# Low halves of streamed weights: a VectorE subtraction against a ScalarE negative with a DMA that adds

## The chip, the core and the metric

The kernel runs on one core of a Trainium2 chip. The metric is the device time of one execution in microseconds (us). The engines are named as the profile names them: PE is TensorE (PEld its weight loads), DVE is VectorE, ACT is ScalarE, POOL is GpSimd, SP is SyncE, which issues nearly all DMAs.

## What is computed

One layer of a decoder trunk with 1024 tokens and a model width of 1024, all in float32. A normed input is projected to six streams; an S5 branch (a complex diagonal state space model) and an RG-LRU branch (a causal convolution, two gates per head, a linear recurrence) run side by side; their outputs are merged by sigmoid gates, projected by `w_out`, normed, added to the input, and a gated projection of a second input `p` is added. Cut to what matters here, which are the products with weights:

```python
h = rms_norm(x, g_pre)
s5_x, s5_g, lru_x, lru_g, gate_s, gate_l = jnp.split(h @ w_in, IN_SPLITS, axis=-1)
y_s = s5_ssm(s5_x, ...)
glu_a, glu_b = jnp.split(jax.nn.gelu(y_s) @ w_glu, 2, axis=-1)
z_s = (glu_a * jax.nn.sigmoid(glu_b) * jax.nn.silu(s5_g)) @ w_bs
y_l = rg_lru(causal_depthwise_conv(lru_x, conv_w, conv_b), w_a, b_a, w_x, b_x, lam)
z_l = (y_l * jax.nn.silu(lru_g)) @ w_bl
merged = jax.nn.sigmoid(gate_s) * z_s + jax.nn.sigmoid(gate_l) * z_l
x = x + rms_norm(merged @ w_out, g_post)
x = x + (p @ w_ple) * jax.nn.sigmoid(x @ w_ple_gate)
```

## The kernel before

**Products in halves.** A float32 product is made of three fast ones. Each operand is split into a high half, which is the value rounded to the format of TensorE's fast mode (float32r), and a low half, which is the rest. `three` (L307) issues high x high (L309), high x low (L310) and low x high (L311) into one PSUM bank, each a matmul of 128x128 weights with 512 columns.

**The weight stream.** All weights lie in DRAM as 128x128 blocks in the order of use. `weight_plan` makes 207 quads of them, up to four blocks each (16 quads have two). SP loads them in chunks of up to eight blocks into four raw buffers (`wraw`, and one small buffer for chunks of two blocks). `make` (L212) gives each quad a slot of a ring of six (`wq`): ScalarE copies the raw quad into the high half (L221), rounding it. The low half is owed: `lows` (L225) lets VectorE subtract the high half from the raw quad (L228). `ahead`, called before each quad is used, converts up to four quads ahead, then lets the low halves follow up to one quad behind that, then fetches chunks up to eight quads further, then forms sums two quads further. `fetch` (L165) issues a chunk's load in the program only when a raw buffer's last quad has been converted and is no longer owed.

**Sums of quads.** The products with `w_bs` and `w_out` use Strassen's scheme, in which some weights are sums of blocks: S1, S2, S3, S4. GpSimd forms them (`sum`, L178 to L210; the add at L193). S1 and S2 have one tile each, S4 is written over S2, and S3 over a raw buffer. For `w_out` four quads form a group, S2, S3, S1 and S4, and a group's S1 and S2 are formed only once the group before has been converted (L185).

**The stages**, by their time in the profile: start, `p @ w_ple`, the first norm, and the S5 inputs (0 to 100 us); 18 output rows of `w_in` with the S5 scan as background work (100 to 290); ten heads of the RG-LRU (290 to 575); the S5 gates, `w_glu` and `w_bl` (575 to 750); `w_bs` by Strassen (750 to 793); `w_out` by Strassen (793 to 871), where each of four groups has the products oY, oZ, oW and oV; the norm and `w_ple_gate`, first for one half of the tokens, then for the other (871 to 993). Background work is written as generators, and `tick` takes one step of each after a quad's matmuls.

**Order.** The order of the instructions on PE, DVE, ACT and POOL is that of the code, and each engine takes its own in that order; SP's DMAs are ordered as they are issued in the program. An instruction that waits holds up all behind it on its engine. Waits are set by the framework from what each instruction reads and overwrites: a ring slot may be rewritten when TensorE has used it, a raw buffer or a sum's tile when its readers are done.

Of the kernel before, what the change touches and what calls it, by code (L numbers as in the profile page):

```python
# [9 lines left out]
F32 = mybir.dt.float32  # L10
F32R = mybir.dt.float32r
I32 = mybir.dt.int32
AF = mybir.ActivationFunctionType
ALU = mybir.AluOpType
# [121 lines left out]
class Weights:  # L136
    RING = 6
    RAW = 4

    def __init__(self, ctx, tc, src):  # L140
        self.nc = tc.nc
        self.src = src
        self.rawp = ctx.enter_context(tc.tile_pool(name="wraw", bufs=self.RAW))
        self.tmp = ctx.enter_context(tc.tile_pool(name="wtmp", bufs=1))
        self.ring = ctx.enter_context(tc.tile_pool(name="wring", bufs=self.RING))
        self.raws = {}
        self.live = [[], []]
        self.loads = 0
        self.fetched = 0
        self.ready = []  # L150
        self.done = []
        self.owed = []
        self.sums = {}
        self.pos = 0
# [10 lines left out]
    def fetch(self, upto):  # L165
        while self.fetched <= min(upto, len(QUADS) - 1):
# [3 lines left out]
            live = self.live[small] = [i for i in self.live[small] if i >= len(self.done) - len(self.owed)]  # L170
            if need + len(live) > (1 if small else self.RAW):
                return
# [39 lines left out]
    def make(self, upto):  # L212
        nc = self.nc
        while len(self.done) <= min(upto, len(QUADS) - 1):
            i = len(self.done)
            self.sum(i)
            src, n = self.ready[i]
            t = self.ring.tile([P, 2, 4, P], F32R, tag="q", name=f"wq{i}")
            hi = t[:, 0].rearrange("p b m -> p (b m)")[:, :n * P]
            lo = t[:, 1].rearrange("p b m -> p (b m)")[:, :n * P]  # L220
            nc.scalar.activation(hi, src, AF.Copy)  # L221
            self.owed.append((i, lo, src, hi))
            self.done.append(t)

    def lows(self, upto):  # L225
# [1301 lines left out]
```

## Time and profile before

| what | value |
|---|---|
| time, median of 3 runs | 996.49 us (992.3 to 997.97) |
| the profiled execution, its own time | 995.16 us |
| its span, first to last instruction | 993.4 us |
| granted TensorE clock, mean | 0.988 |
| L228, the subtractions, of `wraw` and of sums | 189 and 18, 135.6 and 13.3 us busy |
| L221, the copies, of `wraw` and of sums | 189 and 18, 110.6 and 11.3 us busy |
| bytes moved by DMA | 114.56 MB, mean 115 GB/s |

A page of the profile lists busy time per engine, then groups of instructions by line: what is written and read, the count, the busy time, the mean duration in ns, the idle time of the engine ahead of them and what ended it. The chain of work that ended last is followed back from the last instruction to what released each step; its shares say on whom the time was spent. A line of a table of stages has the stretch in us from the span's start, its length, then for each engine busy time and instructions. The engine is named in a row of a timeline behind its start and duration; in brackets stands how long the engine sat idle and for whom.

### The profile page before, as it was taken

To read this page: it belongs to the slowest core of one execution; us is meant where nothing else is said; L and a number is where in the kernel's file an instruction comes from. 1 tells how busy PE (TensorE), PEld (TensorE's weight loads), DVE (VectorE), ACT (ScalarE), POOL (GpSimd) and SP (SyncE) were. 2 spreads that over 40 slices of the span, in tenths; PEclk is the share of its full clock that TensorE was granted. 3 is DMA by queue.
4 is the path that set the end of the run, shared out by engine and by line. 5 is a ranking of instruction groups with operands and counts; after the bars stand their busy time and mean duration, and the time that the engine had idled before them with its cause. 6 is when DMAs were issued, how large, how long until landed. Compare 5 with 4: busy or idle time off the path is not lost.

```text
span 993.4 us, 11730 instructions
## 1 busy us (share of the span) xinstructions
PE 953.5 (96%) x4280; PEld 777.8 (78%) x4280; DVE 654.9 (66%) x1129; ACT 437.0 (44%) x622; POOL 136.5 (14%) x133
## 2 busy tenths in 40 slices
PE   7899999999999999999999999999999977999998
PEld 5688777888788888888888888888887755887777
DVE  7753777888751336666666666345626998898853
ACT  7552244334432256777776664122312234436331
POOL 0255411211100000000000000000102255311200
PEclk9899999999999999999999999999999999999989
DMA  9634232333243111111111134722633626345451
GB/s 348 234 76 127 91 99 83 112 113 112 75 123 109 62 48 48 48 48 48 48 48 48 48 90 156 277 87 69 203 131 131 207 66 212 95 146 163 145 174 64
DMA packets 59099, 114.56 MB, mean 115 GB/s; under 512 B 17824, under 2 KB 28448, under 8 KB 59040
## 3 DMA queue, kind: packets, MB, share of 16 engines
q1 hardware_dynamic: 59040, 113.80, 35.6%
q8 instruction: 34, 0.56, 0.2%
q14 instruction: 25, 0.20, 0.1%
HBM read 84.81 MB, written 27.79 MB: 113 GB/s over the span
## 4 chain that ended last, share of the span: by engine, by line
PE 74%; DVE 18%; issue 3%; DMA 2%; ACT 1%; POOL 1%; SPq 0%; DVEq 0%; ACTq 0%; POOLq 0%
PE ps_L L309 4%; PE ps_L L311 4%; PE ps_L L310 4%; PE ps_rg L311 4%; PE ps_rx L311 4%; PE ps_rx L309 4%; PE ps_rg L309 4%; PE ps_rg L310 4%; PE ps_rx L310 4%; PE ps_bl L309 4%; PE ps_bl L311 4%; PE ps_bl L310 4%; DVE wq L228 3%; PE ps_pg L310 2%; PE ps_pg L311 2%
## 5 line engine op out<-in xcount | busy, mean ns | idle before, releaser
L228 DVE TENSOR_TENSOR wq<-wraw,wq 128x512 fp32r<-128x512 f32 (+1 forms) x189 | 135.6, 732 | 26.6 <-ACT wq L221 26.5
L221 ACT ACTIVATE wq<-wraw 128x512 fp32r<-128x512 f32 (+1 forms) x189 | 110.6, 606 | 65.8 <-PE ps_bl L311 41.0
L309 PE MATMUL ps_L<-hB,wq 128*128 128x512 f32 x320 | 127.2, 397 | 0.0
L311 PE MATMUL ps_L<-hB,wq 128*128 128x512 f32 x320 | 124.7, 390 | 0.0
L310 PE MATMUL ps_L<-hB,wq 128*128 128x512 f32 x320 | 124.6, 390 | 0.0
L193 POOL TENSOR_TENSOR wS<-wraw 128x512 f32<-128x512 f32 x6 | 14.3, 2379 | 464.2 <-DMA wraw<-w_blocks 440.0
L309 PEld LDWEIGHTS ps_L<-hB,wq 128*128 128x128 f32 x320 | 60.1, 188 | 13.4 <-issue 1.7
L311 PEld LDWEIGHTS ps_L<-hB,wq 128*128 128x128 f32 x320 | 60.1, 188 | 12.9
L310 PEld LDWEIGHTS ps_L<-hB,wq 128*128 128x128 f32 x320 | 60.2, 188 | 11.8
L1034 DVE SCALAR_TENSOR_TENSOR c<-ps_rx,cp_t,c 128x1023 f32<-128x1023 f32 (+2 forms) x30 | 38.5, 1282 | 43.6 <-ACT c L1032 42.9
L309 PE MATMUL ps_rx<-hB,wq 128*128 128x512 f32 x160 | 62.5, 391 | 0.0
L309 PE MATMUL ps_rg<-hB,wq 128*128 128x512 f32 x160 | 62.5, 391 | 0.0
L311 PE MATMUL ps_rx<-hB,wq 128*128 128x512 f32 x160 | 62.4, 390 | 0.0
L311 PE MATMUL ps_rg<-hB,wq 128*128 128x512 f32 x160 | 62.4, 390 | 0.0
L309 PE MATMUL ps_bl<-yl,wq 128*128 128x512 f32 x160 | 62.3, 389 | 0.0
L311 PE MATMUL ps_bl<-yl,wq 128*128 128x512 f32 x160 | 62.3, 389 | 0.0
L310 PE MATMUL ps_rx<-hB,wq 128*128 128x512 f32 x160 | 62.2, 389 | 0.0
L310 PE MATMUL ps_rg<-hB,wq 128*128 128x512 f32 x160 | 62.2, 389 | 0.0
L310 PE MATMUL ps_bl<-yl,wq 128*128 128x512 f32 x160 | 62.2, 389 | 0.0
L310 PE MATMUL ps_pg<-x1hl,wq 128*128 128x512 f32 x120 | 48.6, 405 | 3.0 <-DVE x1hl L1223 1.6
L309 PE MATMUL ps_pg<-x1hl,wq 128*128 128x512 f32 x120 | 48.2, 402 | 1.3 <-ACT x1hl L1216 1.3
L311 PE MATMUL ps_pg<-x1hl,wq 128*128 128x512 f32 x120 | 48.0, 400 | 0.7 <-DVE wq L228 0.7
(418 smaller groups left out, 2137.1 us busy)
## 6 DMA issues: line engine op xcount, KB each, us to landing
wraw<-w_blocks SPq DMA_DIRECT2D x90, 512.0 KB, 4.1
xt<-x_t SPq DMA_DIRECT2D x8, 512.0 KB, 7.4
ple_d<-ple_sb SPq DMA_DIRECT2D x8, 512.0 KB, 8.2
sgl_d<-sg SPq DMA_DIRECT2D x8, 512.0 KB, 4.9
sgs_d<-sg SPq DMA_DIRECT2D x8, 512.0 KB, 4.0
blg<-sgl_d SPq DMA_DIRECT2D x8, 512.0 KB, 4.5
ms_d<-blg SPq DMA_DIRECT2D x8, 512.0 KB, 3.5
gsp<-sgs_d SPq DMA_DIRECT2D x16, 256.0 KB, 4.1
```

Of the source, the lines that this page charges most:

```text
L193: G.tensor_tensor(s[name], s[a], s[b], op)
L221: nc.scalar.activation(hi, src, AF.Copy)
L228: self.nc.vector.tensor_tensor(lo, src, hi.bitcast(F32), ALU.subtract)
L309: T.matmul(ps, wh, xh, start=start, stop=False, skip_group_check=more)
L310: T.matmul(ps, wh, xl, start=False, stop=False, skip_group_check=more)
L311: T.matmul(ps, wl, xh, start=False, stop=stop, skip_group_check=more)
L1034: V.scalar_tensor_tensor(c[:, d:], ps[:, :NT - d], w_[3 - d], c[:, d:], ALU.mult, ALU.add)
```

## The change

For quads from the ninth on (`ON_CHIP = 8`), no subtraction is owed. ScalarE writes a second copy of the quad, multiplied by -1 and rounded to the same format, into the low half. Then GpSimd issues a DMA that reads the raw quad and adds it onto what stands there: w - high. The result is the same low half.

```diff
     RING = 6
     RAW = 4
+    ON_CHIP = 8
...
             nc.scalar.activation(hi, src, AF.Copy)
-            self.owed.append((i, lo, src, hi))
+            if i < self.ON_CHIP:
+                self.owed.append((i, lo, src, hi))
+            else:
+                nc.scalar.activation(lo, src, AF.Copy, scale=-1.0)
+                nc.gpsimd.dma_start(lo.bitcast(F32), src, accum_op=ALU.add)
             self.done.append(t)
```

Lines behind the first added one are numbered one higher, and those behind `make` five higher, in the changed kernel: the add of `sum` is L194, the copies are L222, the negatives L226, the DMAs L227, the remaining subtractions L233. As `owed` stays empty after the eighth quad, `fetch` sees a raw buffer as free as soon as its quads have been converted in the program, so some weight loads are issued earlier in SP's order.

The order of the instructions at three places, word for word; what an instruction waits for stands in brackets (engines, DMAHW for DMAs issued by SP, DMASW for those issued by GpSimd).

GpSimd in the `w_out` stage, before, from the last sum of the first group to the second group's (`wS_153` and `wS_157` are the tiles of S1 and S2 of the two groups, S4 in that of S2):

```order
L193 TENSOR_TENSOR wS_153_5945<-wraw_5859,wS_153_5945 128x512 [waits DVE_49,Activation_49]
L193 TENSOR_TENSOR wS_157_6066<-wraw_5980 128x512 [waits DMAHW1_49,DVE_49,Activation_49]
L193 TENSOR_TENSOR wS_157_6068<-wS_157_6066,wraw_5978 128x512 [waits DMAHW0_49,DVE_49,Pool_49]
L193 TENSOR_TENSOR wraw_5980<-wraw_5978,wraw_5980 128x512 [waits DMAHW2_49]
L193 TENSOR_TENSOR wS_157_6068<-wraw_5978,wS_157_6068 128x512 [waits DVE_49]
L193 TENSOR_TENSOR wS_161_6162<-wraw_6102 128x512 [waits DMAHW3_49,DVE_49]
```

The same place after the change:

```order
L194 TENSOR_TENSOR wS_153_6094<-wraw_5978,wS_153_6094 128x512 [waits DMASW1_49]
L227 DMA wq_6182<-wS_153_6092 128x512 [waits DMASW5_49,PE_49,Activation_49]
L227 DMA wq_6211<-wS_153_6094 128x512 [waits PE_49,DMASW6_49,Activation_49,Pool_49]
L194 TENSOR_TENSOR wS_157_6219<-wraw_6090 128x512 [waits DMAHW1_49,DMASW3_49]
L194 TENSOR_TENSOR wS_157_6221<-wS_157_6219,wraw_6088 128x512 [waits DMAHW0_49,DMASW4_49,Pool_49]
L194 TENSOR_TENSOR wraw_6090<-wraw_6088,wraw_6090 128x512 [waits DMASW7_49,DMASW0_49]
L227 DMA wq_6251<-wS_157_6221 128x512 [waits PE_49,Activation_49,Pool_49]
L227 DMA wq_6270<-wraw_6090 128x512 [waits PE_49,Activation_49,Pool_49]
L194 TENSOR_TENSOR wS_157_6221<-wraw_6088,wS_157_6221 128x512 [waits DMASW5_49]
```

Before, GpSimd's queue held sums alone, which waited for VectorE or ScalarE where they overwrite a tile. Now the issues of the accumulating DMAs stand between them, each behind ScalarE's negative, and the sums wait for DMAs of that kind (DMASW).

VectorE at the same place, before (`mT` and `mB` are operands of the products, split in two like the weights):

```order
L1223 TENSOR_TENSOR mT_5964<-mg_5558,mT_5963 128x512
L1214 CAST mT_6049<-mg_5556 128x512
L1223 TENSOR_TENSOR mT_6050<-mg_5556,mT_6049 128x512 x2
L1214 CAST mT_6049<-mg_5556 128x512
L1223 TENSOR_TENSOR mT_6050<-mg_5556,mT_6049 128x512
L228 TENSOR_TENSOR wq_6034<-wS_153_5943,wq_6034 128x512
L228 TENSOR_TENSOR wq_6062<-wS_153_5945,wq_6062 128x512
L1223 TENSOR_TENSOR mT_6050<-mg_5556,mT_6049 128x512
```

And after the change:

```order
L1228 TENSOR_TENSOR mT_6113<-mg_5688,mT_6112 128x512 x4
L1219 CAST mT_6198<-mg_5686 128x512
L1228 TENSOR_TENSOR mT_6199<-mg_5686,mT_6198 128x512 x2
L1219 CAST mT_6198<-mg_5686 128x512
L1228 TENSOR_TENSOR mT_6199<-mg_5686,mT_6198 128x512 x2
L1219 CAST mB_6236<-mg_5689 128x512
```

The subtractions for `wq` have left VectorE's queue; the splits of the operands follow each other directly.

SP in the stage of the S5 scan, around the load of `U`, which TensorE needs for the scan's inputs. Before:

```order
L162 DMA wraw_1286<-w_blocks 128x1024 [waits DMAHW0_49,DVE_49,Activation_49]
L993 DMA sgl_d<-sg_1279 128x1024 [waits DMAHW1_49,Activation_49]
L162 DMA wraw_1398<-w_blocks 128x1024 [waits DMAHW2_49,DVE_49]
L905 DMA U_1382<-u_d 128x4x128 [waits DMAHW3_49,PE_49]
L974 DMA y_d<-ysb_1370 128x512 [waits DMAHW4_49,Activation_49]
L993 DMA sgl_d<-sg_1391 128x1024 [waits DMAHW5_49,Activation_49]
```

After:

```order
L163 DMA wraw_1232<-w_blocks 128x1024 [waits DMASW7_49,DMAHW0_49,DMASW6_49,Activation_49]
L998 DMA sgl_d<-sg_1298 128x1024 [waits DMAHW1_49,Activation_49]
L163 DMA wraw_1351<-w_blocks 128x1024 [waits DMASW1_49,DMAHW2_49,DMASW0_49,Activation_49]
L910 DMA U_1403<-u_d 128x4x128 [waits DMAHW3_49,PE_49]
L979 DMA y_d<-ysb_1391 128x512 [waits DMAHW4_49,Activation_49]
L998 DMA sgl_d<-sg_1412 128x1024 [waits DMAHW5_49,Activation_49]
```

The load of a raw chunk ahead of `U` waited for VectorE's subtraction; it now waits for the landing of two accumulating DMAs.

## The prediction

> **What bounds the kernel now.** I read the page's first part, then busy time by stage, then the chain of work that ended last, then the timelines of the one stage where the chain is not on TensorE.
>
> ```profile
> PE 953.5 (96%) x4280; PEld 777.8 (78%) x4280; DVE 654.9 (66%) x1129; ACT 437.0 (44%) x622; POOL 136.5 (14%) x133
> ```
>
> TensorE is busy for 953.5 of 993.4 us, so about 40 us is all that better feeding can return. Busy time and instructions by stage (PE, PEld, DVE, ACT, POOL, then granted clock, DMA share, GB/s) show where they are:
>
> ```profile
> core 0: us, PE busy (x) PEld busy (x) DVE busy (x) ACT busy (x) POOL busy (x), PEclk, DMA share, GB/s
> 0.00:100.00 100.00, 91.05 (x385) 73.12 (x386) 60.37 (x182) 51.02 (x71) 33.19 (x62) 0.97 0.58 195
> 100.00:290.00 190.00, 183.72 (x929) 150.84 (x928) 144.82 (x382) 72.60 (x111) 38.11 (x32) 1.00 0.33 101
> 290.00:575.00 285.00, 285.00 (x1261) 235.07 (x1260) 165.76 (x175) 166.09 (x205) 0.00 (x0) 1.00 0.19 56
> ...
> 750.00:793.00 43.00, 40.11 (x167) 32.50 (x168) 38.54 (x58) 12.72 (x23) 10.51 (x7) 0.96 0.56 184
> 793.00:836.00 43.00, 31.37 (x122) 23.18 (x121) 40.23 (x52) 16.54 (x31) 23.82 (x12) 0.96 0.43 145
> 836.00:871.00 35.00, 34.78 (x144) 27.98 (x145) 31.84 (x45) 14.79 (x27) 14.06 (x10) 0.95 0.33 107
> 871.00:902.00 31.00, 28.81 (x129) 22.42 (x128) 28.78 (x49) 12.54 (x22) 5.66 (x4) 1.00 0.39 119
> 902.00:950.00 48.00, 44.99 (x196) 36.24 (x196) 41.76 (x69) 24.49 (x42) 5.21 (x4) 0.95 0.54 168
> ```
> ```profile
> 575.00:600.00 25.00, 25.00 (x111) 20.59 (x110) 15.62 (x15) 19.57 (x23) 0.00 (x0) 1.00 0.30 86
> ```
>
> A full stage issues 111 matmuls in 25 us, one per 0.225 us: a quad with both halves of the columns (24 matmuls) lasts 5.4 us, one with a single half (12) 2.7 us. From 290 to 575 TensorE has no idle time, and a faster VectorE can give nothing. From 793 to 836 it issues 122 matmuls where 191 would fit, while VectorE is busy 40.23 of 43 us: VectorE is the bound there. The chain agrees, over 0 to 290, 750 to 871 and 871 to 950:
>
> ```profile
> by line: PE ps_L L309 8.4%; PE ps_L L310 8.1%; PE ps_L L311 8.0%; DVE wq L228 5.5%; DMA U<-u_d 5.3%; PE ps_u L310 4.8%; PE ps_u L311 4.7%; PE ps_u L309 4.6%; issue 3.5%; DVE q L948 3.0%; PE pin L927 2.4%; DVE tb L893 2.1%; DVE ta L892 2.1%;
> ```
> ```profile
> by line: DVE wq L228 10.3%; issue 10.0%; DVE mT L1223 8.4%; DVE gsp L1251 8.0%; DVE mB L1223 6.0%; POOL wS L193 6.0%; DVE mg L1253 3.6%; DVE ftp L409 3.5%; PE oY L311 2.9%; PE oY L309 2.4%; PE oY L310 2.3%; PE oW L311 2.3%; PE oZ L311 2.3%;
> ```
> ```profile
> by line: PE ps_pg L310 17.0%; PE ps_pg L311 15.7%; PE ps_pg L309 15.4%; DVE mix L1407 7.8%; DVE x L1408 7.8%; DVE wq L228 6.8%; issue 5.3%; DVE mix L1456 4.0%; DVE x1hl L1223 3.3%; DMA out_t<-sbp 2.4%; PE pst_post L445 2.3%; PE psb_post L46
> ```
>
> The low halves (L228) are 10.3% of 121 us = 12.5 us of the chain between 750 and 871, and 6.8% of 79 us = 5.4 us after it.
>
> **The change, part by part.** 199 of the 207 quads (all but the first eight) lose a VectorE subtraction and get a second ScalarE copy and an accumulating DMA from GpSimd.
>
> ```profile
> L228 DVE TENSOR_TENSOR wq<-wraw,wq 128x512 fp32r<-128x512 f32 (+1 forms) x189 | 135.6, 732 | 26.6 <-ACT wq L221 26.5
> L221 ACT ACTIVATE wq<-wraw 128x512 fp32r<-128x512 f32 (+1 forms) x189 | 110.6, 606 | 65.8 <-PE ps_bl L311 41.0
> ```
>
> *Removed:* 199 x 0.73 = 145 us of VectorE work. *Added on ScalarE:* 199 x 0.61 = 121 us. I cost it at nothing as work: the fullest stage, 290 to 575, goes from 166 to about 198 of 285 us, and 902 to 950 from 24.5 to about 34 of 48. As latency it is one copy, 0.6 us, before each low half can start.
>
> *Added on DMA: the round trip R*, from GpSimd's issue to the landed low half. The trace has no accumulating DMA and none from GpSimd. The nearest rows, issue to landing:
>
> ```profile
> mlp<-ms_d SPq DMA_DIRECT2D x16, 256.0 KB, 3.3
> U<-u_d SPq DMA_DIRECT2D x8, 256.0 KB, 4.6
> toep<-kt SPq DMA_DIRECT2D x8, 32.0 KB, 2.0
> ```
> ```profile
> 0.00:25.00 25.00, 19.49 (x65) 14.40 (x66) 18.20 (x77) 17.79 (x23) 1.30 (x9) 1.00 0.93 348
> ```
>
> Below, R is 2.0 us (32 KB between SBUF tiles). A plain 256 KB load takes 3.3 to 4.6. At 348 GB/s for a share of 0.93, all engines together move 374 GB/s, so 256 KB is 0.70 us; a second read of 256 KB makes R 4.0 to 5.3. The upper end is 7 us, 4.6 doubled in everything but the 2.0 of a small transfer. I take 4.5, nearest to mlp with the second read. The Trainium skill, page "DMA: Bandwidth & Descriptors", section "Anatomy of one DMA — SWDGE (gpsimd) path", fits 2.0 us plus bytes over 436 GB/s for a DMA of this kind, which would make R 2.6 us. By that the sum below would be 11 us lower; the plain rows of this trace are already slower, so I don't use it.
>
> *Where R is hidden.* Quads are converted four ahead. The tightest steady place is the gate stage at the end:
>
> ```profile
> 973.13 1.15 ACT L221 ACTIVATE wq<-wraw 128x512 fp32r<-128x512 f32 x2
> ```
> ```profile
> 983.32 0.28 PE L309 MATMUL ps_pgz<-x1hl,wq 128*128 128x256 f32 x1
> ```
>
> The last two quads are converted by 974.3 and used from 983.3: with the two negatives between, the last low half is started by 975.5, 7.8 us ahead. R = 4.5 is hidden, and so is any up to about 7.5 us. Earlier stages, at 5.4 us per quad, have more.
>
> *Where it is not hidden: the Strassen loop of w_out (793 to 871).* Its quads are sums that GpSimd forms in tiles with one buffer, and four quads repeat: S2, S3, S1, S4. The next S2 may overwrite its tile only after the low half of S4 has read it, and S4 only after that of S2. These waits move from a VectorE subtraction to a landed DMA. They now stand in GpSimd's own queue, and the issues for S3, S1 and S4 are queued behind them. The rows of before, for the second group:
>
> ```profile
> 824.90 0.66 ACT L221 ACTIVATE wq<-wS 128x512 fp32r<-128x512 f32 x1
> ...
> 835.37 0.63 ACT L221 ACTIVATE wq<-wS 128x512 fp32r<-128x512 f32 x1 [7.80 <-POOL wS L193]
> ```
> ```profile
> 827.52 6.48 POOL L193 TENSOR_TENSOR wS<-wraw 128x512 f32<-128x512 f32 x1 [6.17 <-DVE wq L228]
> 834.08 1.26 POOL L193 TENSOR_TENSOR wS<-wS,wraw 128x512 f32<-128x512 f32 x1
> ...
> 851.59 1.68 POOL L193 TENSOR_TENSOR wS<-wraw 128x512 f32<-128x512 f32 x1 [3.02 <-DVE wq L228]
> 853.35 1.63 POOL L193 TENSOR_TENSOR wS<-wS,wraw 128x512 f32<-128x512 f32 x1
> ```
> ```profile
> 836.05 0.53 PE L309 MATMUL oY<-mT,wq 128*128 128x512 f32 x1 [3.27 <-ACT wq L221]
> ```
>
> Today GpSimd's sum waits 6.17 us for VectorE, then takes 6.48 us instead of some 1.3 beside a VectorE without a gap, and TensorE stands until 836.05. The chain from 759 to that conversion:
>
> ```profile
> by line: issue 17.1%; DVE gsp L1251 14.7%; DVE wq L228 14.4%; DVE mT L1223 13.0%; DVE mB L1223 11.1%; DVE mg L1253 6.7%; DVE ftp L409 6.4%; DVE mg L1290 3.7%; DVE mtmp L1292 3.2%; DVE Fu L418 3.1%; DVE gsp L1268 2.3%; DVE Fu L398 1.8%; DVE
> ```
>
> 14.4% of 66 us is 9.5 us of L228, all on VectorE's own queue, so after the change S4 of the first group is converted some 9 us earlier than 824.90. That is 816; its negative is ready at 817, its low half lands at 817+R, S2 is summed (1.4) and copied twice (1.3), and its low half lands at 819.7+2R = 828.7, instead of 837. But each further group costs two such rounds: 2 x (1.4+1.3+R) = 5.4+2R = 14.4 us, where TensorE needs 4 x 2.7 = 10.8. The fourth group (sums at 851.59 and 853.35, first used at 860 today) is two groups later: 819.7+2R+10.8+4R = 830.5+6R = 857.5. So this stage wins only about 3 us of its 12.5: most of VectorE's relief is handed to the loop. At R = 5 it wins nothing, at 3.3 it wins 10, at 7 it loses 12.
>
> *After 871:* 5.4 us of L228 on the chain; TensorE, with 2.2 and 3.0 us idle in the two stages, is next. I take -5 (bounds 0 and -7, with the half-clock stretches that follow idle time).
>
> *100 to 290:* TensorE idles 6.3 us in all; the two waits behind it are
>
> ```profile
> PE pin L927 <- DMA U<-u_d: 3.6, 3, 1.8
> PE pwin L909 <- DVE ta L894: 2.6, 4, 1.3
> ```
>
> Both lie behind VectorE: the load of U stands in SP's queue behind a weight load that waits for a low half. In the change it waits for a landing instead. I take half, -3 (bounds +3, if GpSimd's queue, held by s5_out_weights, delays those landings, and -6). *Start:* one L228 of 1.37 us at 43.21 leaves the chain, -1 (bounds +1 and -3).
>
> *DMA load:* in the gate stage, one accumulate per 2.7 us.
>
> ```profile
> 950.00:975.00 25.00, 25.00 (x107) 20.52 (x106) 11.96 (x19) 7.46 (x14) 0.00 (x0) 0.95 0.50 162
> ```
>
> A share of 0.50 is 1.35 us of each 2.7. An accumulate costs 0.7 us if it is a plain copy, 1.4 with two full reads: 2.75 us against 2.7, just full. I take two reads and +2 over the 32 gate quads (bounds 0 and, at four copies' worth, 2.8 us, +45).
>
> **Sum:** -3 -5 -3 -1 +2 = -10. The profiled execution took 995.16 us (span 993.4 and 1.8 around it), 1.3 below the median of 996.49; so **985 us**.
>
> **Rivals.**
> *The DMA engines become the bound (slower).* If an accumulate holds the engines for more than 1.35 us, the gate stage runs at their pace. For: nothing in the trace limits its price, and weight loads, ple rows and stores already take half. Against: 0.70 us for a plain 256 KB. At three copies' worth, 2.1 us, each of 32 quads lasts 3.45 instead of 2.7: +24, and R grows in the loop (+3), so 985+25 = **1010**.
> *The loop is slow (no change).* R = 7 in the Strassen stage gives +12 instead of -3 there: **1000**. For: the DMA share is 0.43 there already. Against: 3.3 us for mlp, whose loads run in the stages from 750 on beside a share of 0.56.
> *The relief arrives whole.* R near 3.3: -10 there, -6, -5 and -2 elsewhere, nothing for DMA load: **972**.
> *GpSimd's issues are held up by VectorE (slower).* The row of 6.48 us shows a GpSimd instruction stretched by 5.2 beside a busy VectorE. If issuing is stretched alike, R is 9.7 and the loop ends at 830.5+58 = 889 instead of 860: **1015**. The Trainium skill, page "SBUF — State Buffer", section "Who interferes with whom", says that descriptor generation is shut out while VectorE runs in a 2-port mode, but that a subtraction with two SBUF inputs takes only the reading side. By that the stretch of an add says little of an issue; no run here shows which.
> *VectorE's place is taken by ScalarE,* whose in-order queue now carries two copies per quad: the gains vanish, **994**. Against: 16.54 of 43 us busy in the worst stage.
>
> **Chances.** Forecast 0.42 (0.36 of it faster by over 0.5%, about what a measurement of this kernel can tell from no change); DMA bound 0.24; slow loop 0.14 (half slower, half same); whole relief 0.10; ScalarE 0.06; stretched issue 0.04. Faster 0.46, same 0.20, slower 0.34. The range, 968 to 1022, reaches from just under the whole relief to past the DMA-bound case.
>
> **What would show it.** L228 falls to 8 pieces and VectorE below 520 us; ScalarE rises to some 558. Right: the chain from 750 to 871 shows GpSimd, landings and wq copies in place of VectorE, with 14 to 15 us between the sums of one group and the next, and TensorE unbroken from 290 to 740. Wrong: landings over 7 us, a DMA share near 1 after 900, or waits of ps_pg for the accumulating DMA.

## The result, and the profile after

The changed kernel takes 1011.4 us (median of 4 runs, 1008.0 to 1013.3), the kernel before 996.7 beside it. The ratio is 1.015, 95% interval 1.011 to 1.019: **slower by 1.5%**, where 985 us was forecast. The profiled execution has a span of 1009.1 us, before 993.4.

The first part of the page after, engines by busy time, and the DMA queue that GpSimd feeds (packets, MB, share of 16 engines):

```profile
PE 959.3 (95%) x4280; PEld 782.0 (77%) x4280; DVE 546.6 (54%) x930; ACT 534.4 (53%) x821; POOL 294.0 (29%) x332
...
q0 software_dynamic: 28656, 50.08, 29.0%
```

VectorE lost 108 us of busy time and ScalarE gained 97, where the prediction had 145 and 121. The stages after, in the columns of the prediction's tables:

```profile
100.00:290.00 190.00, 182.05 (x921) 150.50 (x920) 133.91 (x379) 83.59 (x133) 60.36 (x59) 0.98 0.57 146
290.00:575.00 285.00, 285.00 (x1261) 235.06 (x1261) 135.00 (x120) 192.51 (x263) 48.34 (x56) 1.00 0.46 104
...
793.00:836.00 43.00, 32.09 (x117) 23.77 (x115) 38.25 (x48) 19.73 (x38) 21.91 (x19) 0.86 0.69 176
836.00:871.00 35.00, 27.14 (x97) 20.70 (x98) 11.33 (x17) 11.08 (x20) 17.80 (x17) 0.88 0.74 186
...
902.00:950.00 48.00, 47.74 (x215) 38.75 (x215) 37.47 (x60) 34.51 (x61) 20.88 (x21) 1.00 0.97 244
```

From 836 to 871 TensorE issues 97 matmuls, 144 before, though VectorE, busy for 32 of these 35 us before, now is for 11: it is no longer what TensorE waits for. The longest waits of TensorE and of GpSimd from 790 to 900 us (total, times, longest) are now:

```profile
PE oW L316 <- DMA wq<-wS: 9.8, 4, 4.0
PE oY L316 <- DMA wq<-wS: 5.2, 3, 2.5
```
```profile
POOL wS L194 <- DMA wq<-wS: 16.8, 6, 4.4
```

Of the 21.8 us that TensorE waits in these 110 us (13.9 before), 15.0 are for the landing of the accumulating DMAs of the Strassen sums.

For all kernels the table gives the *lag*: the start of the same matmul (high x high) in that kernel's trace less its start in the trace of before, in us. Each row rests on one traced execution. The marks are the first matmuls of quad 16 (third of the 18 `w_in` rows), quad 38 (fourteenth row), quad 151 (end of oX), quad 156 (oV of the first `w_out` group), quad 168 (oV of the fourth) and quad 199 (gate stage, second half). The version with the gate stage alone has the code of before up to quad 168, and yet runs 3 us ahead from quad 16 on: read the differences along a row, not a single number. In rows that have the code of before in the stretch, the lag changes by up to 3.2 us up to quad 16, by up to 1.0 from 16 to 38 and by up to 0.4 from 151 to 168.

| kernel | 16 | 38 | 151 | 156 | 168 | 199 | end |
|---|---|---|---|---|---|---|---|
| changed | 8.9 | 4.6 | 2.2 | 10.5 | 21.1 | 15.5 | 15.8 |
| VectorE in the w_out groups | 9.5 | 5.1 | 2.6 | 3.9 | 5.1 | -0.9 | -0.7 |
| DMA in the w_out groups alone | -3.2 | -4.2 | -4.2 | 4.0 | 13.2 | 13.5 | 13.7 |
| sums in place | 6.0 | 1.8 | 1.3 | 8.0 | 9.7 | 3.2 | 3.4 |
| DMA from quad 44 on | 0.1 | 0.5 | 0.4 | 8.0 | 20.7 | 14.5 | 14.8 |
| plain copy | 6.4 | 1.5 | -2.1 | 2.3 | 5.4 | -3.5 | -3.2 |
| no DMA | -6.5 | -12.4 | -13.6 | -14.9 | -15.1 | -25.4 | -25.4 |
| DMA in the gate stage alone | -3.2 | -3.2 | -3.1 | -3.2 | -3.0 | -8.9 | -8.6 |
| quads 14, 15 by VectorE | -0.2 | -4.5 | -5.8 | 1.8 | 11.8 | 6.7 | 7.0 |
| in place, x from ScalarE | 7.4 | 3.0 | 2.7 | 4.9 | 5.9 | 11.8 | 12.0 |
| load that nobody waits for | 1.1 | -2.5 | -5.9 | -5.3 | -3.6 | -8.4 | -8.1 |
| S5 and gate stage by DMA | -0.9 | -5.0 | -5.0 | -5.0 | -4.6 | -11.8 | -11.6 |
| the same and quads 147 to 152 | 0.7 | -3.4 | -6.3 | -5.9 | -5.5 | -11.0 | -10.8 |

The changed kernel loses 4.6 us up to quad 38, 18.9 in the `w_out` groups (quad 151 to 168), and gains 5.3 behind them.

The 18.9 us are more than the waits. From quad 151 to 168, before and after, in the columns of the tables above:

```profile
805.60:868.30 62.70, 51.94 (x206) 39.77 (x205) 57.03 (x79) 27.38 (x50) 31.19 (x17) 0.95 0.39 130
807.70:889.30 81.60, 59.80 (x205) 44.05 (x204) 45.02 (x58) 37.02 (x69) 43.73 (x39) 0.85 0.65 157
```

TensorE's idle time grows by 11.0 us, from 10.8 to 21.8. Its busy time grows by 7.9 for as many matmuls, at a granted clock of 0.85 instead of 0.95: behind a wait of 4.03 us that ends at 835.92, ten matmuls take 0.63 to 0.80 us each, and those from 840.8 on 0.39. How much of the 7.9 would otherwise have been more waiting, no run here shows.

**The w_out loop.** Here the groups wait for each other. GpSimd's timeline of the third group and the start of the fourth, after:

```profile
854.27 1.29 POOL L194 TENSOR_TENSOR wS<-wraw 128x512 f32<-128x512 f32 x1 [4.17 <-DMA wq<-wS]
855.64 1.30 POOL L194 TENSOR_TENSOR wS<-wS,wraw 128x512 f32<-128x512 f32 x1
...
858.67 0.88 POOL L227 DMA_DIRECT2D wq<-wS  x1 [0.46 <-POOL wraw L194]
...
862.53 1.29 POOL L194 TENSOR_TENSOR wS<-wraw,wS 128x512 f32<-128x512 f32 x1 [1.74 <-DMA wq<-wS]
863.77 0.86 POOL L227 DMA_DIRECT2D wq<-wS  x1
865.54 0.86 POOL L227 DMA_DIRECT2D wq<-wS  x1 [0.91 <-issue]
870.76 1.28 POOL L194 TENSOR_TENSOR wS<-wraw 128x512 f32<-128x512 f32 x1 [4.36 <-DMA wq<-wS]
872.12 1.28 POOL L194 TENSOR_TENSOR wS<-wS,wraw 128x512 f32<-128x512 f32 x1
```

S2 is summed at 855.64 and next at 872.12: 16.5 us a group. The issue for S2 is at 858.67, those for S1 and S4 at 863.77 and 865.54. What these three took to land, from the DMA issues of 858 to 859, 863 to 864.5 (with the loads of raw chunks issued there) and 865 to 866:

```profile
wq<-wS POOLq DMA_DIRECT2D x1, 256.0 KB, 3.8
```
```profile
wraw<-w_blocks SPq DMA_DIRECT2D x2, 512.0 KB, 5.4
wq<-wS POOLq DMA_DIRECT2D x1, 256.0 KB, 6.9
```
```profile
wq<-wS POOLq DMA_DIRECT2D x1, 256.0 KB, 6.4
```

The landing of S3's low half and the sum of S4 free the group's raw buffers, so SP's next two chunks, 1 MB, start in the same microsecond as S1's low half, and S1 and S4, which also overlap each other, take longer to land. So a period is 2 x (1.3 for a sum + 1.7 for two copies and two hand-overs) + 3.8 + 6.4 = 16.2.

### The profile page after: what moved, and what is told of

Its sections match the earlier page's. It is cut to its first block, busy times and chain, and to the rows that moved or that the text cites. A ratio compares the mean times of both kernels' runs of the same rounds, so it can differ in the third digit from the quotient of the medians.

```text
span 1009.1 us, 12313 instructions
## 1 busy us (share of the span) xinstructions
PE 959.3 (95%) x4280; PEld 782.0 (77%) x4280; DVE 546.6 (54%) x930; ACT 534.4 (53%) x821; POOL 294.0 (29%) x332
## 5 line engine op out<-in xcount | busy, mean ns | idle before, releaser
L227 POOL DMA_DIRECT2D wq<-wraw x181 | 158.2, 893 | 568.8 <-ACT wq L226 528.3
L222 ACT ACTIVATE wq<-wraw 128x512 fp32r<-128x512 f32 (+1 forms) x189 | 114.2, 605 | 40.3 <-DMA wraw<-w_blocks 15.5
L226 ACT ACTIVATE wq<-wraw 128x512 fp32r<-128x512 f32 (+1 forms) x181 | 108.8, 601 | 0.0
L995 ACT ACTIVATE sg<-ps_L 128x1024 f32<-128x1024 f32 x20 | 20.5, 1027 | 55.4 <-PE ps_L L316 41.1
L314 PE MATMUL ps_pg<-x1hl,wq 128*128 128x512 f32 x120 | 47.8, 398 | 0.8 <-ACT x1hl L1221 0.8
L315 PE MATMUL ps_pg<-x1hl,wq 128*128 128x512 f32 x120 | 47.8, 398 | 0.8 <-DVE x1hl L1228 0.8
```

Source lines behind the costliest of these rows:

```text
L226: nc.scalar.activation(lo, src, AF.Copy, scale=-1.0)
L227: nc.gpsimd.dma_start(lo.bitcast(F32), src, accum_op=ALU.add)
L314: T.matmul(ps, wh, xh, start=start, stop=False, skip_group_check=more)
L315: T.matmul(ps, wh, xl, start=False, stop=False, skip_group_check=more)
L995: S.activation(t, ps, AF.Sigmoid)
```

## The experiments

In the mixed versions one condition chooses VectorE's subtraction, and `fetch` counts a buffer as in use from the first owed quad on:

```diff
-  i >= len(self.done) - len(self.owed)
+  i >= (self.owed[0][0] if self.owed else len(self.done))
```

**Where the loss sits: the w_out groups by VectorE, and the counterpart.**

```diff
-            if i < self.ON_CHIP:
+            if i < self.ON_CHIP or 153 <= i <= 168:
```

> The sixteen quads of the w_out groups (153 to 168) get their low halves from VectorE again; the other 183 quads keep the negative and the DMA. Theory L (the loss sits in the w_out groups, where sums wait for landings): between the first oX in question and the fourth oV the changed kernel fell back from +2 to +21 us; that goes, the +2 of the earlier stages and the -5.5 of the gate stage stay, so 997 + 2 - 5.5 = 993 to 994 us. Theory D (the accumulating DMAs load the DMA engines everywhere, and the groups only show it): the load outside the groups is as it was, so the time stays above 1004.

Measured: 992.6 us, ratio to before 0.997 (0.995 to 0.999). The lag grows by 2.5 us from quad 151 to 168 instead of 18.9. The counterpart has `if not 153 <= i <= 168`:

> The counterpart: only the sixteen quads of the w_out groups get the negative and the DMA, all others VectorE's subtraction. Theory L: the +19 of the groups comes back nearly whole, less some 2 to 4 us since the stage starts without the delay of GpSimd's queue, and nothing is gained in the gate stage: 1010 to 1016 us. Theory D: 16 accumulates of 256 KB are too few to load anything, so 996 to 1000.

Measured: 1011.9 us, ratio 1.018 (1.014 to 1.021). These sixteen of the 199 DMAs alone make a loss as large as the whole one; theory L holds in both.

**What makes the landing a wait: sums in place.** S1 goes over A22 and S4 over A12 in the raw buffers, so only S2 keeps a tile:

```diff
-                add("S1", "A21", "A22", ALU.add)
+                add("S1", "A21", "A22", ALU.add, "A22" if q[0] == "O2" else None)
-                add("S4", "A12", "S2", ALU.subtract, "S2")
+                add("S4", "A12", "S2", ALU.subtract, "A12" if i > 152 else "S2")
```

> All as in the changed kernel, but in the w_out groups S1 is formed in the raw buffer of A22 and S4 in that of A12, so no sum of the next group waits for a landing of the group before, and S4 doesn't wait for the landing of S2. Theory L1 (the single tiles are what turns the landing into a wait): groups 2 to 4 run at TensorE's 11 us instead of 16, which returns some 5 us for each of the three, 12 to 15 in all: 996 to 999 us. What is left there is the first group (S1 and S4 landing in 8 us, beside the loads of x). Theory L2 (the latency of one landing and the two in-order queues of ScalarE and GpSimd are slow whatever the tiles): under 4 us come back, above 1007.

Measured: 1000.2 us, ratio 1.006 (1.003 to 1.008), just above the range of L1: 10.5 of the 18.9 us come back, not 12 to 15. Groups 3 and 4 add nothing to the lag (9.7 at oZ of the second group and at the fourth's oV), where the changed kernel goes from 10.4 at the second group's oV to 21.1. Yet the low halves of the third group's S2, S3 and S1 still take 7.1 to 7.6 us to land: it is the waiting for them that costs. So L1 holds; the first group's 6.7 us stay.

**The loads of x.** The kernel with sums in place, and `nc.scalar.dma_start` for the eight loads of x:

> The kernel with S1 and S4 formed in place (1000.2 us), with the eight loads of x (512 KB each) issued from ScalarE's queue, which reaches them only at the fourth w_out group, instead of SP's, which runs ahead and issues them beside the first group. Theory X (what is left in the first two groups are landings of 7 to 8 us beside these 4 MB): those landings fall to 3.5 to 6.5 us and 3 to 5 us come back: 995 to 997. Rival: the landings of the raw chunks alone hold the groups, or x now comes late for the norm: 999 or more.

Measured: 1008.0 us, ratio 1.012 (1.009 to 1.015). Both theories had a part: the lag grows by 3.2 us in the groups instead of 8.4, but then x comes late. The waits of ScalarE and TensorE from 870 to 905 us:

```profile
ACT sq L1344 <- DMA x<-x_t: 10.7, 1, 10.7
...
PE pst_post L450 <- DVE ssq L1349: 9.2, 1, 9.2
```

So the loads of x do lengthen the landings: in the second group all four low halves now land in 3.3 to 3.7 us, against 6.3 to 8.1 with sums in place and x from SP. In the changed kernel it is the first group's S1 and S4 that land beside x, in 7.9 and 8.4 us. But this was not the way to move these loads.

**The S5 stage: the DMA from quad 44 on, then two quads alone.** `if i < 44`:

> DMA halves only from quad 44 on (the RG-LRU heads and later); start and S5 stage as before the change. Theory Q (the 9 us by which the first products after the S5 inputs start late come from two accumulating DMAs that stand in GpSimd's queue behind the preparation of the S5 weights, while SP holds a weight load and the stores of U behind them): that delay is gone, TensorE reaches the heads at the time of before, and the end comes 2 to 4 us earlier than the changed kernel: 1007 to 1009. If the delay had another source in the change, no more than 1 us of it goes: 1010 to 1012.

Measured: 1007.7 us, ratio 1.013 (1.011 to 1.015); the lag at quad 16 is 0.1. In the changed kernel these rows (ScalarE, GpSimd, SP, VectorE) stand behind it:

```profile
81.56 0.62 ACT L226 ACTIVATE wq<-wraw 128x512 fp32r<-128x512 f32 x1
```
```profile
88.82 1.29 POOL L731 TENSOR_TENSOR bb<-bb,braw 128x512 f32<-128x512 f32 x1
90.05 1.76 POOL L227 DMA_DIRECT2D wq<-wraw  x2
```
```profile
95.03 0.33 SPq L163 DMA_DIRECT2D wraw<-w_blocks  x1
95.47 4.71 SPq L819 DMA_DIRECT2D u_d<-up  x3
```
```profile
102.64 0.06 DVE L857 MEMSET tt<- 128x2 f32 x1 [23.87 <-DMA u_d<-up]
```

The negatives are there by 82.2, but GpSimd takes the two DMAs only at 90.05, behind the preparation of the S5 weights (L731 is its last line). SP's weight load waits for their landing, the stores of U wait behind it in SP's queue, and VectorE stands for them until 102.64. Before the change it went on ten us earlier:

```profile
92.52 0.06 DVE L852 MEMSET tt<- 128x2 f32 x1 [12.88 <-ACT wq L221]
```

To pin it on those two, `if i < self.ON_CHIP or i in (14, 15)`:

> As the changed kernel, but quads 14 and 15 get their low halves from VectorE. Theory Q of the S5 stage, pinned down: these are the two whose DMAs stood in GpSimd's queue behind the preparation of the S5 weights (ready on ScalarE by 82 us, issued at 90), while SP held a weight load and the stores of U until they had landed. From the first matmul of quad 16's output (65 to 70 us) to the first one of the row after the S5 inputs (115 to 124 us) the kernels without those two DMAs took 46 to 47.5 us, those with them 52 to 55; here it should be 46 to 49. One look, so the whole time is not the point: 1006 to 1011. If another DMA or the load in general was the cause, it stays at 52 or more.

The two marks meant there, at 65 to 70 and 115 to 124 us, are the first matmuls of quads 8 and 16. Between them the changed kernel took 53.7 us, before 47.5, this one 46.0. Its time is 1002.2 us in a single run, below the 1006 to 1011 expected, and VectorE goes on at 93.81:

```profile
93.81 0.06 DVE L857 MEMSET tt<- 128x2 f32 x1 [12.91 <-DMA u_d<-up]
```

From quad 16 to 38 it gains 4.3 us, as the changed kernel did: that is VectorE's relief, and the two stuck DMAs had hidden it.

**What an accumulate costs: a plain copy.** `accum_op=ALU.add` left out:

> As the changed kernel, but GpSimd's DMA is a plain copy of the raw quad into the low half, without the addition (the low half is then w instead of w - high). Issue, queue order and waits stay; a packet of 2 KB should take the 84 ns of plain ones instead of 185, so each quad holds the DMA engines 0.7 us less. Theory C (contention: part of the loss is that loads of mlp and x and the landings lengthen each other): landings of mlp around 790 fall from 8 to 9 us to under 6, the w_out groups get 1.5 us shorter each, 5 to 8 us in all: 1003 to 1007. Theory Q (only latency and in-order queues count): under 2.5 us, above 1008.

Measured: 987.9 us, ratio 0.992 (0.990 to 0.994), far below what theory C asked. GpSimd's issues (count, busy, mean ns), the queue, and the median landings:

```profile
L227 POOL DMA_DIRECT2D wq<-wraw x181 | 98.2, 543 | 617.9 <-ACT wq L226 561.0
```
```profile
q0 software_dynamic: 15408, 50.08, 13.3%
```
```profile
wq<-wraw POOLq DMA_DIRECT2D x165, 256.0 KB, 2.6
wq<-wS POOLq DMA_DIRECT2D x18, 256.0 KB, 4.7
```

The changed kernel has 893 ns, 29.0% of a span 1.02 times as long for the same bytes, and

```profile
wq<-wraw POOLq DMA_DIRECT2D x165, 256.0 KB, 3.9
wq<-wS POOLq DMA_DIRECT2D x18, 256.0 KB, 6.4
```

So an accumulate holds the DMA engines 2.2 times as long, GpSimd 0.35 us longer, and lands 1.3 to 1.7 us later (medians). Along the row the gain lies in the groups (7.5 us instead of 18.9), up to quad 38 (3.1) and behind the groups (3.3 more). What I had wrong in theory C is the place: mlp still took 6.5 us around 790, 7.8 in the changed kernel and 2.9 before.

**Relief without a landing: no DMA.** ScalarE writes w times 2^-12, the DMA is left out:

> As the changed kernel, but with no DMA at all: ScalarE writes the high half, and as low half w times 2^-12; the addition is left out. It shows what freeing VectorE and charging ScalarE is worth when no landing has to be waited for. Theory: the whole relief of the prediction, -10 in the w_out stage, -5 to -6 behind it, -3 in the S5 stage: 975 to 980. Rival: the second copy in ScalarE's queue takes back most of it: 988 or more.

Measured: 972.0 us, ratio 0.976 (0.974 to 0.978), more than expected, and elsewhere: 12.4 us come by quad 38 (of which some 3 may be scatter) and 10.3 behind the groups, but only 1.5 in the groups. GpSimd's and VectorE's timelines while the operands of the first group are made:

```profile
795.74 1.77 POOL L1295 TENSOR_TENSOR mg<-mg,mg 128x512 f32<-128x512 f32 x1 [1.24 <-DVE mg L1294]
```
```profile
794.98 0.68 DVE L1294 TENSOR_TENSOR mg<-mg,mg 128x512 f32<-128x512 f32 x1
795.69 0.69 DVE L1296 TENSOR_TENSOR mtmp<-mg,mg 128x512 f32<-128x512 f32 x1
796.30 1.75 DVE L1227 TENSOR_TENSOR mT<-mtmp,mT 128x512 fp32r<-128x512 f32 x1
797.98 0.68 DVE L1294 TENSOR_TENSOR mg<-mg,mg 128x512 f32<-128x512 f32 x1
```

Each block takes 3.0 us in turns of the two engines, 1.75 of it a split beside GpSimd's 1.77. No subtraction is left there, and yet the pace is that of the kernel before (whose line L1290 is L1294 here):

```profile
809.89 0.68 DVE L1290 TENSOR_TENSOR mg<-mg,mg 128x512 f32<-128x512 f32 x1
...
812.89 0.68 DVE L1290 TENSOR_TENSOR mg<-mg,mg 128x512 f32<-128x512 f32 x1
```

**Load that nobody waits for.** The kernel without DMA, with two plain copies to DRAM in its place:

```diff
-                nc.gpsimd.dma_start(lo.bitcast(F32), src, accum_op=ALU.add)
+                for j in range(2):
+                    nc.gpsimd.dma_start(self.load_d[(2 * i + j) % 8][:, :n * P], lo.bitcast(F32))
```

> The kernel without DMA (972 us; low half w times 2^-12, the addition left out), with load on the DMA engines that nobody waits for: for each of the 199 quads GpSimd issues, at the place of the accumulating DMA and behind the same ScalarE copy, two plain copies of the low half to a scratch tile in DRAM (256 KB each, so together about the 1.4 us of all engines that one accumulate takes). GpSimd's queue is held as in the changed kernel. Theory W (the time is lost by waiting for the landing, and load only lengthens that wait): 974 to 982. Rival C (the load delays mlp, x and the raw chunks enough by itself, or GpSimd's held queue does): 990 or more, most of the 39 us to the changed kernel.

Measured: 986.2 us, ratio 0.991 (0.989 to 0.992), between the two theories. The queue's share is a little below the 29.0% of the accumulates:

```profile
q0 software_dynamic: 30816, 100.16, 26.2%
```

As far as two plain copies to DRAM stand for one accumulate, some 14 of the 39 us come from load or from GpSimd's held queue, which this run doesn't tell apart, and 25 from waiting. In the groups the lag grows by 2.3 us, in the changed kernel by 18.9: there it is the waiting. Behind them both gain about 5, half of the 10.3 without load.

**The gate stage alone.** `if i < 169`:

> Negative and DMA only for the 38 quads of w_ple_gate and the last rows (169 to 206); all before as in the kernel before. Theory: from the last oV to 956 us the changed kernel and those with the DMA there gained 5.5 to 7 us on the kernel before, since VectorE is the bound there, so 6 us less than before: 988 to 991 where before is 995 to 997. Rival S (those gains were slack made up after slow w_out groups, VectorE's pending sums being done by then): the time of before within 2 us.

Measured: 987.3 us, ratio 0.993 (0.990 to 0.995): the relief there is real. **With the S5 stage:** `if i < 20 or 43 < i < 169`:

> A mix: negative and DMA for quads 20 to 43 (the S5 stage behind the two stuck DMAs) and 169 to 206 (the gate stage), VectorE for all others. From 124 to 267 us the changed kernel made up 4.3 us on the kernel before, so theory: the 987.3 of the version with the gate stage alone, less 3 to 4: 983 to 985. Rival: what it made up there was only its own late start, and the S5 stage gains nothing: 987 to 989.

Measured: **983.4 us**, ratio 0.988 (0.987 to 0.990), faster than both kernels; 4.1 us come between quads 16 and 38. **And six plain quads before the groups:** `if i < 20 or 43 < i < 147 or 152 < i < 169`:

> The mix of before (quads 20 to 43 and 169 to 206 by DMA; 0.988 of the kernel before) with the six plain quads of the first w_out products, 147 to 152, by DMA too. They are converted from 785 to 806 us, where VectorE is busy without a gap and is what the first w_out group waits for. Theory V (a subtraction taken from VectorE there brings the first group forward): 6 x 0.7 = 4 us less, 979 to 981, ratio 0.983 to 0.985. Rival G (the first sums stand in GpSimd's queue behind these issues, which stand behind ScalarE's negatives and the late mg, so the splits of mT get no earlier): within 2 us of the mix or later, ratio 0.987 to 0.993.

Measured: 983.8 us, ratio 0.988 (0.986 to 0.990): nothing gained, rival G. GpSimd's rows of this kernel, then of the one without the six:

```profile
797.61 0.86 POOL L227 DMA_DIRECT2D wq<-wraw  x1 [0.64 <-ACT wq L226]
798.17 1.62 POOL L194 TENSOR_TENSOR wS<-wraw 128x512 f32<-128x512 f32 x1
```
```profile
792.41 1.74 POOL L194 TENSOR_TENSOR wS<-wraw 128x512 f32<-128x512 f32 x1
```

The first sum stands behind the issue of quad 152 and starts 5.8 us later; it then runs beside the splits of the operands.

## Why the prediction was wrong

*The sign fell in the w_out loop.* Its mechanism was forecast: sums that wait for landings in tiles with one buffer, and VectorE's relief handed to the loop. Three terms of "830.5+6R" were too small. The formula dated the low half of the fourth group's S2 to 857.5; it landed 3.3 us behind its issue at 875.1, so at 878.4, 21 us later.

- *"S4 of the first group is converted some 9 us earlier than 824.90. That is 816."* This step failed. It was converted here:

```profile
829.53 0.65 ACT L222 ACTIVATE wq<-wS 128x512 fp32r<-128x512 f32 x1
```

That is 13.5 of the 21 us. I took L228's share of the chain, 9.5 us, as time that would be saved. The kernel without any DMA shows that the groups gain 1.5: behind the subtractions stands the turn of VectorE and GpSimd over the operands, at the same pace. Taking six subtractions away just ahead of it gained nothing either. It even came 4.6 us later than before, and the rows show why. VectorE and GpSimd, before and then after, where VectorE begins these turns and where GpSimd begins the first group's three sums:

```profile
806.88 0.68 DVE L1290 TENSOR_TENSOR mg<-mg,mg 128x512 f32<-128x512 f32 x1
797.42 1.74 POOL L193 TENSOR_TENSOR wS<-wraw 128x512 f32<-128x512 f32 x1
```
```profile
806.25 2.05 DVE L1295 TENSOR_TENSOR mg<-mg,mg 128x512 f32<-128x512 f32 x1
806.13 1.61 POOL L194 TENSOR_TENSOR wS<-wraw 128x512 f32<-128x512 f32 x1
```

VectorE begins 0.6 us earlier, but the sums now stand behind the issues of quads 151 and 152, and these behind a load of mlp for which GpSimd waited 4.2 us, until 800.09. So the sums run beside VectorE, whose first two operations take 2.05 and 1.64 us instead of 0.7, and S2's issue at 816.81 stands between two further turns: the fourth turn begins 3.6 us later than before. The last 1.0 us are two negatives ahead of S4's copy on ScalarE.

- *"R = 4.5".* With no load beside it an accumulate of a sum lands in 3.3 to 3.8 us, better than I took; beside the raw chunks in 6.3 to 6.9, beside x in 7.9 and 8.4. I had one R for all, and did not ask what the landing itself sets free: the chunks that collide with the next landings. The late S4 of the first group accounts for some 4 us.
- *"2 x (1.4+1.3+R) = 14.4"* was 15.8 and 16.5 (S2's sums start at 839.8, 855.6 and 872.1), from a mean R of 5.1 and 0.3 us of hand-over in each half: 3.5 us over two groups.

*100 to 290, -3 (bounds +3 and -6):* the bound I named was GpSimd's queue held by `s5_out_weights`. It was held, but earlier, by the preparation of the S5 weights that ends with L731, and for more than the +3: 6.2 us between quads 8 and 16. The relief behind it, -4.3, was forecast well. Two DMAs of 199 decided the sign of this stage.

*After 871, -5, and DMA load, +2:* together -3, measured -5.3 behind the groups and -5.6 with the gate stage alone. The price of an accumulate, two full reads, was right (2.2 copies' worth). Both terms were too small: without DMA the stage gains 10.3, and the plain copy gains 3.3 more there than the accumulate.

*Start, -1:* a loss of 2.8 us at quad 8, where versions with the code of before differ from it by up to 1.9; not settled. *ScalarE's second copies at nothing:* nearly right. The kernel that has them without DMA is the fastest of all, and the only place where I saw them on the path is the 1.0 us ahead of S4.

*The rivals.* The one called "the loop is slow", R = 7 there, came nearest: its +12 was 18.9. The DMA engines becoming the bound gave the right time, 1010, for a reason that did not occur, since the gate stage got faster: at a DMA share of 0.97 TensorE is busy 47.74 of 48 us. "The relief arrives whole" gave 972, which the kernel without DMA takes, but by gains in other stages than that sum had. By its own terms the rival of the stretched issue comes to some 1017 us, not 1015, and the chances add up to 0.19 for the same and 0.35 for slower; neither changes a reading. Issues were not stretched by VectorE by anything like 5.2 us: their row (min, median, max in ns) is

```profile
L227 POOL DMA_DIRECT2D wq<-wraw x181: 804/862/1502, 45.3 to 991.1; - x181
```

*What would show it:* L228 fell to 8 pieces and TensorE ran unbroken from 290 to 750. VectorE stayed at 546.6, over 520, since other work on it took longer: L865 24.6 us, 14.9 before, and L809 14.0, 5.6 before. In the kernel without DMA it was no lower than 541 either. Of the signs of being wrong, landings over 7 us came true for S1 and S4 of the first group, and a DMA share near 1 after 900 came true without harm; ps_pg hardly waited.

## What to carry to other kernels

An engine's share of the chain is not what its removal saves: look for the next sequence that runs at the same pace beside it, and test it by leaving the work out. When a subtraction becomes a DMA, ask of each quad whether its source has a buffer of its own, what its landing sets free, and which in-order queue its issue stands in; apply it where the cover is long (here the S5 and gate stages, -1.2%) and not where a buffer goes round in a loop.

## What the runs showed of the hardware

An accumulating DMA between SBUF tiles costs 2.2 times a plain copy of the same 256 KB on the DMA engines (29.0% against 13.3% of the span for 50 MB), and 0.89 against 0.54 us of GpSimd. The Trainium skill, page "DMA: Bandwidth & Descriptors", section "Anatomy of one DMA — SWDGE (gpsimd) path", fits 2.0 us plus bytes over 436 GB/s, which makes an estimate of 2.6 us for 256 KB: the plain copy's median here is just that, the accumulate's is 3.9. A DMA share of 0.97 over 48 us left TensorE busy for all but 0.3 of them, while an accumulate issued in the same microsecond as two loads of 512 KB landed in 6.9 us instead of 3.8. I had expected the first to hurt more and had not looked for the second.
